# Rotary tables multiplied out on chip, n1 and pooled tiles in pairs, fold drains of 512 columns, and other scheduler constants: one change to an encoder kernel on eight cores

## The chip, the cores and the metric

One Trainium2 chip, all eight cores, each with two of the sixteen sequences and no traffic between cores. The metric is device time in microseconds of the slowest core. The chip has a second, slower state: in some executions the cores of one die run at a mean granted clock down to 0.83, the other die's stay at 0.99, and the time is 2276 to 2593 us, whatever the kernel. Such executions are left out here. Because the slowest of eight cores is a noisy figure, I also give the **mean of the eight cores** of one execution, averaged over the fast executions of a kernel.

## The reference

```python
n1 = rmsnorm(x, g_mix)
proj = n1 @ w_in                      # q, k, v, pooled branch, two gates
a = gqa_block_attention(rope(rms(q)), rope(rms(k)), v) @ w_attn_up
p = (multiscale_pool(u) @ pool_w * pool_scale) @ w_pool_up
h = x + (sig(g_a) * a + sig(g_p) * p) @ w_out
h = h + cross_attention(rmsnorm(h, g_cross), rmsnorm(mem, g_mem))   # 4 heads, 256 memory tokens
h = h + relu(rmsnorm(h, g_ffn) @ w_ff1) ** 2 @ w_ff2
return rmsnorm(h, g_final)
```

A sequence of 2048 is a grid of 32 rows and 64 columns; the rotary angle of half the dimensions follows the row, of the other half the column. So cos and sin tables are products of a row table and a column table.

## The kernel before

The program is written as a graph of operations. A list scheduler, run when the kernel is built, gives every operation to an engine and fixes the order on each engine, from a small model of what each costs. All loads and stores are issued by SyncE (SP), one queue, in the scheduled order. Eight blocks of 512 tokens pass; the raw f32 weights come in 228 loads of 512 KB (`wst`), are rounded to bf16 in one of ten W slots, and are stored to scratch (`wsc`) for the later blocks. The parts that the change touches:

```python
DMA_BW = 318.0                        # the scheduler's model of transfers
BACKLOG = 6000.0
...
def rope_tables(tb):
    for i in range(2):
        c = V("cs", "M1")
        load(lambda c=c: ap(c), rope_d[tb, i], 262144, [c], early=30000.0)
...
for kc in range(8):                   # n1 goes out in eight tiles of 128 KB
    store(n1d[s, tb, kc], lambda n=n: ap(n), 131072, [n], [dram(("n1", s, tb, kc))])
...
def fold_a(h, ch):                    # W_q and K of the memory folded into one matrix
    PE([mm(b, wsl(w, dt * 1024 + ch * 128), m[("XK", 2 * h + dt)], ...) for dt in range(2)], [b])
    for s in range(2):
        copy_any(At[s] [..., ch, :], b[:, s * 256:(s + 1) * 256], 256, ..., scale=g_cross[ch])
```

The softmax here doesn't subtract the row's maximum and nothing guards it: scores larger than these inputs give would overflow.

## Time and profile before

| kernel before | |
|---|---|
| time, slowest core | 2255.9 us median of the three first runs (2252.47 to 2256.78) |
| PE busy in the profiled run | 2140.6 of 2253.9 us, 95% |
| PE idle by stretch: 0-140, 140-260, 260-480, 480-560 us | 33, 22, 8, 12 us |
| period of the steady blocks | 245.7 us |
| moved by DMA, main queue | 440.6 MB |

PE is nearly always busy, so every gain without fewer matmuls must come out of its idle time, and most of that lies in the first 260 us. The lines of this profile are in the prediction.

### The profile page before, as it was taken

Reading aid. Unit: us, or ns where it says so; the run is one execution under the profiler, and the core shown is the slowest. Engines: PE = TensorE matmul, PEld = TensorE weight load, DVE = VectorE, ACT = ScalarE, POOL = GpSimd, SP = SyncE. Lnnn points to the kernel's source line nnn. Section 1 sums busy time; section 2 is a strip of 40 time slices with the busy share of each in tenths; the row PEclk is TensorE's granted clock in tenths of the full one; section 3 lists DMA queues with packets and bytes.
Section 4 is the critical chain, followed back from the end, with each engine's and each line's share of the span. In section 5 each row is a group of like instructions: output and inputs, shape, how many; then the busy total and the mean of one; then the engine's idle time right before and its main releaser. Section 6 shows DMA issues by size and latency. Waiting matters only on the chain.

```text
span 2253.9 us, 33704 instructions; the slowest of 8 cores (2242.3 to 2253.9 us)
## 1 busy us (share of the span) xinstructions
PE 2140.6 (95%) x10758; PEld 900.0 (40%) x10758; DVE 1471.4 (65%) x1793; ACT 1481.2 (66%) x1875; POOL 368.5 (16%) x273
## 2 busy tenths in 40 slices
PE   6788999988999999999999999999999999999997
PEld 3423333333444434444434443444434443444443
DVE  4688876667876687666774578557774687456502
ACT  6678777747786477853788368854786368835550
POOL 0112321124221241101110021002110122000100
PEclk9999999999999999999999999999999999999998
DMA  9957995989587992946633463435533463336342
GB/s 284 287 189 244 299 306 185 286 277 314 199 275 267 284 306 101 299 153 197 211 113 122 151 223 104 139 124 191 174 117 117 168 215 113 123 128 226 127 145 75
DMA packets 156267, 442.75 MB, mean 196 GB/s; under 512 B 17472, under 2 KB 38976, under 8 KB 156096
## 3 DMA queue, kind: packets, MB, share of 16 engines
q1 hardware_dynamic: 156096, 440.60, 60.7%
q8 instruction: 91, 1.49, 0.3%
q14 instruction: 80, 0.66, 0.1%
HBM read 376.57 MB, written 63.96 MB: 195 GB/s over the span
## 4 chain that ended last, share of the span: by engine, by line
PE 81%; DMA 6%; ACT 4%; DVE 4%; issue 3%; SPq 1%; POOL 0%; DVEq 0%; ACTq 0%; POOLq 0%
PE ps L603 81%; DMA M_p<-wst 3%; ACT M_p L1014 2%; DMA wsc<-W_p 1%; SPq L611 1%; DMA outT<-M_p 1%; SPq L615 1%; DMA M_p<-xT 1%; DVE M_p L1270 0%; DMA vec_sb<-vec 0%; ACT M_p L1241 0%; DVE M_p L1025 0%; ACT M_p L709 0%; DVE S_p L715 0%; ACT W_p L623 0%
## 5 line engine op out<-in xcount | busy, mean ns | idle before, releaser
L603 PE MATMUL ps<-S_p,W_p 128*128 128x512 bf16 x7680 | 1731.9, 381 | 33.1 <-DVE S_p L715 7.7
L603 PEld LDWEIGHTS ps<-S_p,W_p 128*128 128x128 bf16 x7680 | 733.7, 98 | 996.2 <-issue 160.3
L1014 ACT ACTIVATE M_p<-ps 128x2048 bf16<-128x2048 f32 x256 | 479.5, 1873 | 220.3 <-PE ps L603 215.9
L1025 DVE TENSOR_TENSOR M_p<-M_p 128x1024 f32<-128x1024 f32 x224 | 284.5, 1270 | 162.2 <-ACT M_p L1014 158.0
L1026 DVE TENSOR_TENSOR M_p<-M_p 128x1024 f32<-128x1024 f32 x224 | 309.6, 1382 | 17.4 <-DVE M_p L1025 0.9
L698 POOL TENSOR_TENSOR M_p<-M_p 128x512 f32<-128x512 f32 x67 | 101.3, 1512 | 806.3 <-ACT M_p L689 710.4
L689 ACT ACTIVATE M_p<-M_p 128x512 f32<-128x512 f32 x216 | 134.1, 625 | 137.2 <-DVE M_p L1222 47.0
L626 POOL CAST W_p<-M_p 128x1024 bf16<-128x1024 f32 x92 | 115.1, 1256 | 493.8 <-PE ps L603 291.8
L1241 ACT ACTIVATE M_p<-ps 128x512 f32<-128x512 f32 x256 | 151.6, 592 | 46.7 <-PE ps L603 45.2
L1257 DVE TENSOR_TENSOR M_p<-ps,M_p 128x512 f32<-128x512 f32 x64 | 44.2, 691 | 208.3 <-PE ps L603 208.3
L603 PE MATMUL ps<-S_p,KV_p 64*128 64x512 bf16 x1024 | 157.1, 385 | 15.4 <-ACT M_p L1014 14.8
L603 PE MATMUL ps<-M_p,KV_p 128*64 128x512 bf16 x1024 | 137.0, 389 | 16.6 <-ACT M_p L1014 12.3
L1245 ACT ACTIVATE S_p<-M_p 128x512 bf16<-128x512 f32 x220 | 138.6, 630 | 20.4
L623 ACT ACTIVATE W_p<-M_p 128x1024 bf16<-128x1024 f32 x71 | 74.4, 1051 | 108.1 <-PE ps L603 88.3
L1092 ACT ACTIVATE M_p<-ps,nbg 128x512 f32<-128x512 f32 x128 | 87.1, 685 | 58.7 <-PE ps L603 57.9
L603 PE MATMUL ps<-W_p,S_p 128*128 128x256 bf16 (+2 forms) x576 | 96.1, 318 | 4.0 <-ACT W_p L623 1.8
L603 PEld LDWEIGHTS ps<-M_p,KV_p 128*64 128x64 bf16 x1024 | 49.3, 110 | 96.7 <-issue 72.2
L626 DVE CAST W_p<-M_p 128x1024 bf16<-128x1024 f32 x61 | 42.7, 716 | 65.4 <-PE ps L603 29.2
L603 PEld LDWEIGHTS ps<-S_p,KV_p 64*128 64x128 bf16 x1024 | 29.6, 94 | 121.4 <-issue 121.3
L603 PE MATMUL ps<-S_p,ones_bf 128*128 128x512 bf16 x166 | 56.5, 403 | 19.0 <-ACT S_p L689 11.6
L603 PEld LDWEIGHTS ps<-W_p,S_p 128*128 128x128 bf16 x576 | 55.1, 100 | 43.6 <-issue 21.3
L1095 ACT ACTIVATE M_p<-M_p 128x1024 f32<-128x1024 f32 x64 | 67.5, 1055 | 4.1
(76 smaller groups left out, 1486.7 us busy)
## 6 DMA issues: line engine op xcount, KB each, us to landing
W_p<-wsc SPq DMA_DIRECT2D x383, 512.0 KB, 4.3
M_p<-wst SPq DMA_DIRECT2D x228, 512.0 KB, 9.8
wsc<-W_p SPq DMA_DIRECT2D x69, 512.0 KB, 9.3
M_p<-xT SPq DMA_DIRECT2D x128, 256.0 KB, 10.6
outT<-M_p SPq DMA_DIRECT2D x64, 256.0 KB, 4.7
M_p<-rope SPq DMA_DIRECT2D x32, 256.0 KB, 10.7
n1d<-S_p SPq DMA_DIRECT2D x56, 128.0 KB, 9.1
S_p<-n1d SPq DMA_DIRECT2D x56, 128.0 KB, 5.6
```

What stands on the lines that cost most here:

```text
L603: return e.matmul(out(), lhsT=lhsT(), rhs=rhs(), start=start, stop=stop, skip_group_check=True, **kw)
L623: return e.activation(out=dst(), in_=src(), func=AF.Copy)
L626: return e.tensor_copy(out=dst(), in_=src())
L689: A(lambda e: e.activation(out=ap(sq), in_=src(), func=AF.Square), 512, False, R, [sq])
L698: TT(lambda e: e.tensor_tensor(out=ap(out), in0=ap(acc), in1=ap(sq), op=ALU.add), [acc, sq], [out])
L1014: A(lambda e: e.activation(out=b16(P).rearrange("p (a n) -> p a n", n=512), in_=ps[:, 0:4, :], func=AF.Exp, scale=0.125), 2048, True, S, [P])
L1025: D(lambda e: e.tensor_tensor(out=ap(acc), in0=ap(acc), in1=lo(), op=ALU.add), 1024, [P, acc], [acc], port=True)
L1026: D(lambda e: e.tensor_tensor(out=ap(acc), in0=ap(acc), in1=hi(), op=ALU.add), 1024, [P, acc], [acc], port=True)
L1092: A(lambda e, b=b, i=i: e.activation(out=ap(Et)[:, i * 512:(i + 1) * 512], in_=ap(b), func=AF.Exp, bias=nbg[:, i * 8 + j:i * 8 + j + 1], s ...
L1095: A(lambda e: e.activation(out=ap(Et), in_=ap(Et), func=AF.Ln, bias=1.0, scale=1.0), 1024, False, [(Et, 0), (Et, 1)], [(Et, 0), (Et, 1)])
L1241: A(lambda e: e.activation(out=ap(rl), in_=ap(b), func=AF.Relu), 512, True, [b], [rl])
L1245: e.activation(out=ap(H), in_=ap(rl), func=AF.Square))
```

## The change

Four things: the rotary tables are no longer loaded but multiplied out from one table of 192 columns; n1 and pooled tiles are moved two at a time; the fold is drained 512 columns at a time for one sample, with its gain moved elsewhere; and the scheduler gets another model of transfers and other rules for SP.

```diff
-DMA_BW = 318.0
-BACKLOG = 6000.0
+DMA_BW = 385.0
+DMA_FIX = 200.0
+BACKLOG = 5000.0
 ...
-if best is not None and r > best[0] + 400.0 and r > s_min + 400.0:
+if best is not None and r > best[0] + (1600.0 if e == "sp" else 400.0) and r > s_min + 400.0:
 ...
-if best is None or c[0] < best[0]:
+if best is None or c[0] < best[0] or (e == "sp" and best[2].dma is not None and c[1] < best[2].U
+                                      and c[0] < best[0] + 1500.0):
 ...
-load(lambda c=c: ap(c), rope_d[tb, i], 262144, [c], early=30000.0)
+TT(lambda e, c=c, i=i: e.tensor_tensor(out=ap(c) as [8 rows, 64 columns],
+    in0=rope[:, row table], in1=rope[:, column table], op=ALU.mult), [CONST["rope"]], [c])
 ...
-for kc in range(8):
-    store(n1d[s, tb, kc], lambda n=n: ap(n), 131072, ...)
+for k2 in range(4):
+    store(n1d[s, tb, k2], lambda v=v: b16(v), 262144, [(v, 0), (v, 1)], ...)
 ...
-for s in range(2):
-    copy_any(..., 256, [b, CONST["vec"]], [(At[s], ch)], scale=g_cross, engs=("act", "dve"))
+copy_any(..., 512, [b], [(At[s], c2)], engs=("act", "dve"))
 ...
-rounded(j, None)
+rounded(j, C_GCROSS)
```

(Cut: the same change for pooled tiles and for the loads; the host's tables; pool sizes M1 24 to 32 and S1 70 to 52; the model of GpSimd's time.)

## The prediction

> **What bounds the kernel now.** I read the page's header first: engines, the forty slices, the chain. TensorE (PE) is busy 95% of 2253.9 us, and the chain runs through it for 81%.
>
> ```profile
> PE 2140.6 (95%) x10758; PEld 900.0 (40%) x10758; DVE 1471.4 (65%) x1793; ACT 1481.2 (66%) x1875; POOL 368.5 (16%) x273
> ...
> PE   6788999988999999999999999999999999999997
> ...
> DMA  9957995989587992946633463435533463336342
> ...
> PE 81%; DMA 6%; ACT 4%; DVE 4%; issue 3%; SPq 1%; POOL 0%; DVEq 0%; ACTq 0%; POOLq 0%
> ```
>
> All that can be won without removing matmuls is PE's idle time, 2253.9 - 2140.6 = 113 us, plus what a lowered clock costs. The slices put the idle time at the start, where the DMA row shows 9s. So next I asked for busy times in seven stretches (columns: PE, weight load, DVE, ACT, POOL, granted clock, DMA share, GB/s):
>
> ```profile
> 0.00:140.00 140.00, 106.84 (x582) 52.71 (x583) 83.64 (x139) 94.72 (x149) 17.21 (x19) 0.91 0.99 289
> 140.00:260.00 120.00, 98.30 (x505) 33.99 (x504) 103.72 (x125) 92.89 (x107) 24.73 (x20) 0.97 0.67 216
> 260.00:480.00 220.00, 211.50 (x1048) 86.35 (x1046) 157.70 (x181) 161.88 (x196) 57.08 (x43) 0.99 0.85 268
> 480.00:560.00 80.00, 67.99 (x309) 28.37 (x309) 59.51 (x81) 54.19 (x68) 28.22 (x22) 0.94 0.97 297
> 560.00:1100.00 540.00, 529.81 (x2775) 231.69 (x2774) 385.79 (x478) 364.83 (x471) 108.56 (x82) 1.00 0.72 233
> 1100.00:2029.00 929.00, 918.30 (x4593) 375.33 (x4591) 598.09 (x674) 617.52 (x743) 119.56 (x80) 1.00 0.44 146
> 2029.00:2254.00 225.00, 207.90 (x957) 91.56 (x955) 82.95 (x119) 95.16 (x143) 13.11 (x10) 0.97 0.43 143
> ```
>
> PE's idle time by stretch is 33, 22, 8, 12, 10, 11 and 17 us. From 1100 to 2029 us, 41% of the run, PE is 99% busy at clock 1.00: nothing in this change removes PE work there, so that stretch should stay. Up to 140 us DMA is 99% busy. From 140 to 260 DMA has room (0.67), but DVE is at 86%; this is attention of the first block beside the fold of W_q and K. The third look was at the waits in 140 to 190 us, and at the groups that drain the fold:
>
> ```profile
> PE ps L603 <- ACT M_p L1014: 10.0, 9, 1.9
> ...
> PE ps L603 <- DVE W_p L627: 3.6, 4, 1.3
> ```
>
> ```profile
> L627 DVE TENSOR_SCALAR W_p<-ps,vec_sb 128x256 bf16<-128x256 f32 x33 | 14.7, 478 | 3.9 <-PE ps L603 2.0 <-DMA wsc<-W_p 1.3
> ...
> L624 ACT ACTIVATE W_p<-ps,vec_sb 128x256 bf16<-128x256 f32 x31 | 13.3, 476 | 3.6 <-DVE W_p L627 1.5 <-DMA wsc<-W_p 1.2 <-PE ps L603 0.4
> ```
>
> There PE waits for the attention exponential on ACT (L1014), which queues behind fold drains, and for drains themselves. The DMA issues show what will go:
>
> ```profile
> M_p<-rope SPq DMA_DIRECT2D x32, 256.0 KB, 10.7
> n1d<-S_p SPq DMA_DIRECT2D x56, 128.0 KB, 9.1
> S_p<-n1d SPq DMA_DIRECT2D x56, 128.0 KB, 5.6
> ```
>
> **What the Trainium skill says.** "Perfetto Trace Analysis", DMA Optimizations, says: "Small DMAs (< 2KB) have significant per-transfer overhead." The n1 and pooled tiles move as 1 KB rows. The trace agrees: in stretches where their stores prevail DMA makes 267 GB/s (50 to 58 us) and 254 (88 to 98), against 320 at 24 to 34 us, at a DMA share of 1.0 throughout. "SBUF — State Buffer", Who interferes with whom, says that GpSimd (POOL) and a DVE instruction with two SBUF inputs contend for a shared port held for a whole instruction. The trace agrees in that the same DVE add L1026 takes 1.23 us mostly but 1.87 once beside a POOL cast (170 us), and its mean is 1.382. "TensorE: Matmul & The Clock Gate", Part 1, has PE at half rate until it has been busy some 3.4 us. Here eight 512-column matmuls took 3.62 us just after a 5.3 us wait (101.9 us) against 1.89 otherwise, and the granted clock at 110 to 120 us was 0.63. "VectorE: DVE Perf Modes", on the TRN2 errata, gives each instruction a fixed part beside its elements. Here a 256-wide drain costs DVE 0.478 us and a 512-wide one 0.684, less than twice; so merging two drains pays.
>
> **The change part by part.**
>
> Rotary tables. Thirty-two loads of 262 KB (8.4 MB of 440.6) become one of 98 KB and 32 products of 128x512. The order of the changed program gives 29 of these to POOL and 3 to DVE. On POOL a 128x512 f32 tensor-tensor takes 1.27 us alone and 1.51 on average (L698): 29 x 1.27 to 1.51 = 37 to 44 us, on an engine 16% busy, on the path only where a rotation waits for its table. On DVE 3 x 0.75 (L1258) = 2.2 us. On the path lies DMA in the first 140 us: ten of the loads fall there, 2.62 - 0.10 = 2.52 MB, at 289 GB/s 8.7 us of queue time. Of the others two fall near 212 us, four at 473 to 536 us, the rest mostly where DMA has room.
>
> Pairs. n1 and pooled moves fall from 168 to 84, each twice as long, rows 2 KB. With the table loads, issues fall by 31 + 84 = 115, from 1084 to 969. In the first 140 us there are 24 + 12 stores of 131 KB, 4.7 MB: at 260 GB/s 18.1 us, at an assumed 305 15.5, so 2.7 us (estimate). M1 grows from 24 to 32 slots and S1 shrinks from 70 to 52. A block's eight n1 and four pooled tiles then take six M1 slots where they took twelve of S1, so prefetch depth hardly changes.
>
> Fold. Per pair of chunks four drains of 256 become two of 512, without the gain. The order gives 14 to DVE and 18 to ACT: 14 x 0.684 + 18 x 0.600 = 20.4 us, against 14.7 + 13.3 = 28.0 by the busy columns (30.5 by count times mean, which keeps overlaps). So 8 to 10 us less on two engines that are both near 85% there, about 4.5 us off the stretch if it shortens evenly. Matmuls rise by 64 but keep their columns: under 1 us. The order also shows 100 fold matmuls in one run, where before an attention visit came after every four to six; PE can stream them but will wait if W_q is late.
>
> Gain moved. The gain g_cross goes into the rounding of h after W_out, 64 instructions that POOL can no longer take. ACT: from 18 x 0.706 + 30 x 0.615 = 31.2 to 70 x 0.706 = 49.4 us, +18.2; DVE 35.4 to 34.8; POOL -15.0. That is 2.3 us more ACT per block, in steps where PE has eight 512-column matmuls per rounding and ACT is near 66%: off the path, apart from some 0.1 us at each stage end.
>
> Scheduler constants. They have SP choose among loads differently and can move any transfer. Two holes in DMA of 20 us (140 to 160 and 340 to 360 us, where SP waited for a slot) could close. The PE order changes throughout, but mode switches hardly: 657 to 653. I give this no sum, only width.
>
> Sum, on the path: first 140 us: 8.7 + 2.7 = 11.4 us of transfers. PE idles 33 us there, of which 14 precede the first projection (18.3 us) and depend on the first x loads, which stay first in the queue. I let 8 of 11.4 through. Clock: 0.91 in that stretch costs 0.09 x 140 = 13 us; fewer long waits may return 2. Fold: 4.5. At 473 to 560 us: four table loads gone, 1.05 MB at 297 GB/s or 3.5 us, and eight n1 and four pooled loads paired, some 0.5 us (estimate): 4. Rest of the head (260 to 480, 560 to 1100): 3. Port contention from 29 products: DVE loses perhaps 29 x 0.3 = 9 us, a tenth of it on the path, -1. Total 8 + 2 + 4.5 + 4 + 3 - 1 = 20.5; 2255.9 - 20.5 = 2235.
>
> **Rivals.** (a) The transfers are hidden anyway: DVE and ACT bound the head once DMA is lighter, only the fold counts. For: DVE at 86% after 140 us. Against: ACT waited 13.7 us and DVE 17.3 for raw weights before 107 us. It gives about 2249. (b) POOL's products hold the shared port and delay DVE in its busiest stretch, and a late table stalls a rotation. For: the 1.23 to 1.87 us spread. Against: POOL is under 21% busy in every early stretch, and tables can be made early. About 2258. (c) The long fold run waits for W_q: eight raw halves must be converted first. For: DMA was saturated until 140 us. Against: the lighter queue brings them some 11 us sooner. About 2245. (d) The new load choice closes the DMA holes as well, and later DMA-bound stretches (240 to 330, 480 to 560 us) start ahead: 15 to 25 us more, about 2215.
>
> **Range and chances.** Idle time outside the steady stretch is 102 us, 14 of it at the very start and 17 in the last stretch, untouched. Faster by over 2% needs 45 us of the remaining 71: only (d) at its best, 0.09. Slower by over 2% needs a new wait in the repeated blocks: 0.02. Within 2%: 0.89. The range 2213 to 2250 holds (a), (c) and most of (d).
>
> **What would show it.** DMA bytes near 432.3 MB, 969 issues. PE idle before 140 us down from 33 to about 23, and the start of the fold about 8 us sooner; fold drains 20 us in all; idle at 480 to 560 us from 12 to about 8; blocks in the steady stretch still 245.7 us apart (1156.66, 1402.34, 1648.00 in the chain). I am wrong if that period moves by over 1 us, if PE waits above 3 us inside the fold run, or if rotations wait on POOL.

## The result, and the profile after

The changed kernel takes **2252.3 us** (median of 4 runs, 2251.99 to 2252.76); the kernel before in the same comparison 2254.18 (4 runs, 2251.19 to 2256.78). The ratio is 0.9992, 95% interval 0.9975 to 1.001. (A ratio is the mean time of one kernel's fast runs over that of the other's of the same rounds, so not quite the ratio of the medians quoted.) The class "same" was right, the size was not: 20 us were predicted, at most 2 came, and 2252.3 lies outside the range of 2213 to 2250.

The page of the changed kernel's slowest core: busy times, the slices of PE and of DMA, what the main queue moved, and the chain by engine.

```profile
PE 2138.2 (95%) x10822; PEld 906.4 (40%) x10822; DVE 1469.2 (65%) x1754; ACT 1492.0 (66%) x1883; POOL 419.4 (19%) x304
...
PE   7978899989999999999999999999999999999997
...
DMA  9976976999496882935633462435533463336342
...
q1 hardware_dynamic: 139536, 432.30, 58.8%
...
PE 80%; DMA 7%; DVE 4%; ACT 3%; issue 3%; SPq 1%; POOL 0%; DVEq 0%; ACTq 0%; POOLq 0%
```

The bytes went as foreseen (432.30 MB), and the DMA row has lost some of its 9s at the front. Its hole moved from 140-160 to 125-141 us. By stretches (columns as in the prediction):

```profile
0.00:140.00 140.00, 112.94 (x655) 56.61 (x656) 102.48 (x151) 101.78 (x154) 44.12 (x39) 0.96 0.89 272
140.00:260.00 120.00, 96.47 (x521) 37.53 (x519) 89.91 (x97) 85.31 (x94) 32.16 (x25) 0.94 0.79 244
260.00:480.00 220.00, 207.78 (x1040) 83.71 (x1037) 158.76 (x179) 163.87 (x198) 50.93 (x38) 1.00 0.80 258
480.00:560.00 80.00, 71.94 (x336) 30.57 (x337) 64.03 (x86) 57.74 (x74) 27.21 (x20) 0.98 0.97 310
```

PE is 6.1 us busier before 140 us (112.94 against 106.84). Then it is 1.8 us less busy to 260 and 3.7 less to 480 us. The gain of the head arrives, and part of it leaks out again. I also looked at the chain of waits from some 90 to 260 us; first the kernel before, then the changed one:

```profile
by line: PE ps L603 54.3%; ACT M_p L1014 10.1%; issue 8.1%; DMA wsc<-W_p 8.1%; DMA M_p<-wst 6.8%; SPq L611 3.6%; DVE W_p L627 3.5%; ACT W_p L623 2.1%; ACT W_p L624 2.0%; DVE W_p L626 1.0%; DVE S_p L1035 0.8%; DVE M_p L1026 0.7%; DVE M_p L10
```

```profile
by line: PE ps L613 44.5%; DMA M_p<-wst 17.2%; ACT M_p L1031 8.9%; issue 6.1%; DMA M_p<-n1d 5.8%; DMA wsc<-W_p 4.1%; ACT W_p L633 4.1%; DVE W_p L636 2.1%; DVE M_p L636 1.5%; SPq L621 1.4%; DVE M_p L1042 1.2%; DVE M_p L1043 0.7%; DVE M_p L75
```

Two things are not to be read out of this pair. The 256-column drains L624 and L627 (5.5%) are not gone but have become 512-column ones on L633 and L636, the lines that also round weights: drains and rounding together hold 8.6% before (L623, L624, L626, L627) and 6.2% after. And the raw weight's transfer, 6.8% against 17.2%, differs as much between the cores of one kernel: it is 27.8% on core 0 of the kernel before, and in the second pair of profiles, r_before and r_after, 6.5 and 7.2%. In the waits at 140 to 190 us, where the prediction had found 10.0 us for the exponential and 3.6 for drains, the changed kernel shows:

```profile
PE ps L613 <- ACT M_p L1031: 8.1, 3, 3.8
PE ps L613 <- DVE W_p L636: 1.1, 3, 0.5
```

Nine short waits for the exponential became three longer ones, with fewer attention visits in the window. (In the second pair of profiles it is 11.1 us in nine waits against 6.5 in four.) The fold itself starts some 10 us sooner, at 133 to 134 us where its first drain came at 143 to 144, and is through at 159 us instead of 187 (means of cores).

**Where the lead goes.** Marks in the traces, mean of the eight cores, each kernel profiled twice (us). The last column is an experiment told below, the kernel before with the rotary bytes taken out at unchanged order.

| mark | before | after | difference | x_bytes, difference |
|---|---|---|---|---|
| first attention exponential of block 0 | 104.8 | 95.5 | -9.3 | -5.4 |
| its 32nd and last | 242.8 | 243.1 | +0.3 | -5.1 |
| end of block 0 | 516.1 | 512.0 | -4.1 | -4.4 |
| end of block 3 | 1313.4 | 1309.4 | -4.0 | -6.4 |
| end, mean of cores | 2244.1 | 2240.3 | -3.8 | -6.4 |

Nine microseconds of lead at the first exponential are nothing at the 32nd and four at the end. The first two rows are clear of the scatter; the lower ones less so, because the two profiles of the kernel before end 6.5 us apart (2247.3 and 2240.8), those of the changed one 0.6. The runs below put the change's gain in the mean of cores at 1.6 us. In the same traces PE's idle time, counted as all gaps of more than 0.45 us up to a time, mean of eight cores and of two profiles:

| up to | 140 us | 200 us | 260 us | 373 us | 480 us | 800 us |
|---|---|---|---|---|---|---|
| before | 27.0 | 40.9 | 46.0 | 51.5 | 55.5 | 64.6 |
| after | 24.3 | 32.8 | 44.7 | 49.2 | 55.7 | 62.3 |
| x_bytes | 23.7 | 36.6 | 42.0 | 47.8 | 54.3 | 60.9 |

At 200 us the changed kernel has saved 8.1 us of idle time. Between 200 and 260 us it gives 6.8 of them back. The threshold matters a little: with every gap counted the lead is 9.0 us at 200, 3.2 at 260, 1.5 at 480 and 3.3 at 800 us.

### The profile page after: what moved, and what is told of

Same layout as the page of the kernel before. It is cut to its first block, busy times and chain, and to the rows that moved or that the text cites. A ratio compares the mean times of both kernels' runs of the same rounds, so it can differ in the third digit from the quotient of the medians.

```text
span 2251.2 us, 33586 instructions; the slowest of 8 cores (2229.4 to 2251.2 us)
## 1 busy us (share of the span) xinstructions
PE 2138.2 (95%) x10822; PEld 906.4 (40%) x10822; DVE 1469.2 (65%) x1754; ACT 1492.0 (66%) x1883; POOL 419.4 (19%) x304
## 3 DMA queue, kind: packets, MB, share of 16 engines
q1 hardware_dynamic: 139536, 432.30, 58.8%
## 4 chain that ended last, share of the span: by engine, by line
PE 80%; DMA 7%; DVE 4%; ACT 3%; issue 3%; SPq 1%; POOL 0%; DVEq 0%; ACTq 0%; POOLq 0%
PE ps L613 80%; DMA M_p<-wst 4%; DMA wsc<-W_p 1%; ACT M_p L1031 1%; SPq L621 1%; DVE M_p L725 1%; DMA outT<-M_p 1%; DMA M_p<-xT 1%; ACT W_p L633 1%; DVE M_p L1286 1%; DMA M_p<-n1d 0%; DVE M_p L636 0%; ACT M_p L720 0%; DVE M_p L1042 0%; DVE M_p L1043 0%
## 5 line engine op out<-in xcount | busy, mean ns | idle before, releaser
L613 PE MATMUL ps<-S_p,W_p 128*128 128x512 bf16 (+1 forms) x6144 | 1370.6, 378 | 19.2 <-ACT W_p L633 5.7
L613 PEld LDWEIGHTS ps<-S_p,W_p 128*128 128x128 bf16 x6144 | 585.0, 98 | 772.2 <-issue 109.8
L613 PE MATMUL ps<-M_p,W_p 128*128 128x512 bf16 x1600 | 380.6, 386 | 10.6 <-DVE M_p L725 5.6
L709 POOL TENSOR_TENSOR M_p<-M_p 128x512 f32<-128x512 f32 x72 | 111.7, 1552 | 811.2 <-ACT M_p L700 778.2
L613 PEld LDWEIGHTS ps<-M_p,W_p 128*128 128x128 bf16 x1600 | 153.9, 99 | 218.2 <-issue 48.5
L636 POOL CAST W_p<-M_p 128x1024 bf16<-128x1024 f32 x96 | 122.0, 1277 | 425.9 <-PE ps L613 232.3
L633 ACT ACTIVATE W_p<-M_p 128x1024 bf16<-128x1024 f32 x71 | 74.1, 1054 | 113.0 <-PE ps L613 73.2
L636 DVE CAST W_p<-M_p 128x1024 bf16<-128x1024 f32 x57 | 42.7, 771 | 57.4 <-DMA M_p<-wst 22.8
L613 PE MATMUL ps<-W_p,M_p 128*128 128x384 bf16 (+1 forms) x512 | 76.9, 305 | 0.0
## 6 DMA issues: line engine op xcount, KB each, us to landing
W_p<-wsc SPq DMA_DIRECT2D x383, 512.0 KB, 4.2
M_p<-wst SPq DMA_DIRECT2D x228, 512.0 KB, 9.0
wsc<-W_p SPq DMA_DIRECT2D x69, 512.0 KB, 8.8
```

Of the source, the lines that this page charges most:

```text
L613: return e.matmul(out(), lhsT=lhsT(), rhs=rhs(), start=start, stop=stop, skip_group_check=True, **kw)
L633: return e.activation(out=dst(), in_=src(), func=AF.Copy)
L636: return e.tensor_copy(out=dst(), in_=src())
L709: TT(lambda e: e.tensor_tensor(out=ap(out), in0=ap(acc), in1=ap(sq), op=ALU.add), [acc, sq], [out])
```

## The experiments

Eighteen kernels ran. First the parts, each alone on the kernel before. "Mean" is the mean of the eight cores over the fast runs; the difference is to the kernel before's fast runs. "Slowest" is the longest core's span, averaged likewise; the device times of which the text gives medians are about 1.5 us longer. "Plan" is the length that the scheduler itself computes while the kernel is built; it is 2224.5 for the kernel before and 2217.5 for the changed one. "96th" is the time at which the 96th raw weight load is issued, and the last column is the end minus that, both means of cores in the profiled run.

| run | what it is | plan | mean | difference | slowest | 96th | end - 96th |
|---|---|---|---|---|---|---|---|
| p_rope | before + rotary products | 2220.1 | 2241.7 | +0.1 | 2249.0 | 375 | 1864 |
| p_pairs | before + pairs | 2214.7 | 2235.9 | -5.7 | 2244.6 | 370 | 1866 |
| p_fold | before + fold | 2223.3 | 2239.1 | -2.5 | 2246.7 | 367 | 1870 |
| p_sched | before + scheduler | 2229.7 | 2249.6 | +8.0 | 2260.5 | 382 | 1869 |
| n_sched | after without scheduler | 2231.9 | 2249.2 | +6.9 | 2259.4 | 375 | 1876 |
| n_fold | after without fold | 2216.3 | 2243.9 | +1.6 | 2255.3 | 377 | 1869 |
| n_rope | after without rotary products | 2213.6 | 2239.5 | -3.7 | 2253.5 | 373 | 1865 |
| r_after | after | 2217.5 | 2240.8 | -1.6 | 2250.5 | 373 | 1867 |
| c_lot | before, model nudged by 0.1 ns | 2227.9 | 2248.0 | +5.7 | 2257.5 | 380 | 1869 |
| x_bytes | before, rotary bytes out, order kept | (2224.5) | 2235.4 | -7.8 | 2245.0 | 373 | 1866 |
| x_bytes2 | the same again | (2224.5) | 2238.9 | -7.0 | 2247.2 | 375 | 1861 |
| r_before | before | 2224.5 | 2242.6 | -0.6 | 2249.9 | 379 | 1862 |
| d_after | after, stores later in SP's order | (2217.5) | 2278.3 | +35.1 | 2288.1 | 411 | 1868 |
| a_s97 | after, model nudged by 2 ns | 2215.9 | 2242.4 | -3.5 | 2251.1 | 373 | 1867 |
| a_s93 | after, model nudged by -2 ns | 2224.3 | 2255.2 | +9.3 | 2263.8 | 388 | 1868 |
| a_m29 | after, model nudged by 0.4 ns | 2217.3 | 2242.9 | -3.0 | 2253.2 | 373 | 1870 |
| p_rope24 | p_rope, model nudged by -0.1 ns | 2211.9 | 2237.1 | -8.8 | 2245.1 | 370 | 1868 |
| a_bytes | after, idle copies added, order kept | (2217.5) | 2274.9 | +29.0 | 2284.1 | 392 | 1882 |

(Two to six fast runs each, p_sched one. The mean of one execution scatters by about 2 us either way. p_sched was in the slow state four times; the undisturbed dies of three of these had means of 2249 to 2252. One fast run of p_sched, 2283.34 us, and one of n_rope, 2277.10, lie far off their own others, with two cores at a clock of 0.97, and are left out of these means. With them the differences would be +11.4 and -2.3; and 2265.12 of n_rope, which shows the same clock, was kept. The 96th load and the end of p_sched are those of its undisturbed die.)

**Each part alone.** The edits are the four parts of the diff above, one each.

> The kernel before with the rotary products alone (tables of 32 and 64 columns multiplied out on chip, nothing else of the change). My prediction's sum put some 8 us on the first 140 us, three quarters of it for these bytes: so if the transfers of the head were the bound and nothing takes it back, the slowest core ends 5 to 8 us sooner, at about 2247 us. If the gain of the head is eaten between the first attention exponential and the end of block 0's attention (as in the whole change, where the first exponential came 10 us sooner and the 32nd at the same time), the first exponential comes about 5 to 8 us sooner and the end is within 3 us. If the rotary products on GpSimd hold VectorE up, the steady blocks are longer by over 1 us each and the end later.

> The kernel before with n1 and pooled tiles in pairs alone. No bytes go, only 92 of the transfers; by the prediction 2 to 3 us of the head. Head-bound theory: end 2 to 3 us sooner. Theory that it only reshuffles the order of the schedule: anything within 5 us either way, with the mean of the eight cores moving as little as the slowest.

> The kernel before with the fold's drains at 512 columns alone (two chunks at a time, one tile of the pair of samples). The prediction gave it 4.5 us plus 2 us of clock. If the drains bound the fold, the end of block 0's attention (mean of cores) comes 4 to 7 us sooner. If the fold waits for raw weights instead (theory of the transfers), the wait moves from the drain lines to the casts of raw weights and the end of block 0's attention stays within 2 us.

> The kernel before with the new constants and rules of the list scheduler alone (transfer rate 385 plus 200 ns each, backlog 5000, SyncE may look 1600 ns ahead, GpSimd's time). The prediction gave it 3 to 4 us of gain at 473 to 560 us and in the rest of the head. Theory that the new constants are too fast for this chip and place casts and loads too early: the chain from 90 to 260 us then carries over 10% on a raw weight's transfer instead of 7%, and block 0's attention ends no sooner or later. Theory that any change of order moves the end by 5 us at random: no pattern.

Measured: medians of 2250.41, 2245.82, 2248.88 and one undisturbed run of 2262.02. The rotary products alone brought nothing where the prediction had most; pairs brought 5.7; the new constants cost 8.0 where 7 of gain had been booked. In p_sched the first exponential came early (96.5 us on the undisturbed die) and the 32nd late (245.8). The four differences sum to -0.1, the whole change has -1.6. (The 92 transfers of the expectation on p_pairs are 84.) At this point the constants looked guilty.

**The whole without one part, and a control.**

```diff
# c_lot, on the kernel before
-MM_FIX = 2.5
+MM_FIX = 2.6
```

> The whole change with the scheduler's old constants and rules. In the first four runs the three other parts each took 1 to 6 us off the mean of the eight cores and off the end of block 0's attention (238 to 240 us against 244), and the new constants alone added some 8 us. If the new constants are what eats the gain, this kernel's mean of cores is 2228 to 2234 us and its slowest core about 2238 to 2243; if the three gains overlap (each removes the same wait), it stays at 2235 to 2238 in the mean; if the long fold run (no attention visit for 19 us) eats it, the run is still there and the mean stays at 2241.

> The whole change with the old fold (256-column drains), new scheduler constants. If the fold's form causes the long run without attention visits and with it the loss, the gap of 19 us in the visits goes and the mean of cores falls from 2241 to 2236 or less. If the scheduler's constants are the cause, the end of block 0's attention stays at 243 us or comes later and the mean stays at 2241 to 2246.

> The changed kernel again, unedited, so that the means of its cores come from the same chip as the other runs: slowest core 2252 us, mean of cores 2240 to 2243, one core of each pair 8 to 15 us behind the other.

> The kernel before with one irrelevant figure of the scheduler's model nudged (a fixed cost per matmul of 2.6 ns instead of 2.5): no work changes, 161 lines of PE's order do. If any nudge moves the end by 5 us or more (lottery), the mean of cores differs from the kernel before's by that much, and the differences of the four parts run so far prove little; if the mean stays within 2 us, they are effects.

Taking the new constants away did not free the gain: n_sched is 8.4 us slower than r_after in the mean. The same constants cost 8 us on the kernel before and win 8 in the changed one, so the theory that they eat the gain by themselves falls. n_fold is not faster either (+1.6). The control is the reason to distrust all of these: a figure of the model nudged by 0.1 ns, no work changed, and the mean is 5.7 us up (ratio 1.003, 1.0012 to 1.0048). Adding a part means a new order of everything, and an order alone is worth as much as a part. What a part is worth has to be measured with the order held.

**The order held.** The loads keep their planned size, so the schedule does not move; a comparison of the instruction lists showed PE, DVE, ACT and POOL the same row by row.

```diff
# x_bytes, on the kernel before (result wrong on purpose)
-load(lambda c=c: ap(c), rope_d[tb, i], 262144, [c], early=30000.0)
+load(lambda c=c: ap(c)[:, 0:32], rope_d[tb, i][:, 0:32], 262144, [c], early=30000.0)
-in1=ap(cs[0])
+in1=ap(cs[0])[:, 0:32].unsqueeze(1).to_broadcast([128, 16, 32])      # and cs[1]
# d_after, on the changed kernel, after scheduling: each scratch store planned before 400 us
+delay_stores(order, 3, 400000.0)   # moves it behind up to 3 later SP issues, if no user comes first
```

> The kernel before in exactly its own order on PE, VectorE, ScalarE, GpSimd and SyncE, with each rotary load cut from 512 to 32 columns (the rotations read those 32 columns again and again; the result is wrong on purpose). The scheduler still plans with the full size, so nothing moves; only the bytes go. By the prediction's term (8 us of the first 140 us, three quarters of it these bytes) the first attention exponential comes 5 to 8 us sooner and the end 5 to 6 us sooner in the mean of the cores. If the transfers are hidden anyway because buffers come free no sooner, the 16th and 32nd raw weight load are issued sooner but the 64th and 96th within 2 us of the kernel before's, and the end within 2 us.

> The kernel before, unedited, for a second profile on the same chip, because the one profiled first was slower (mean of cores 2247 us) than its later executions (2240 to 2244): first attention exponential at 105 us, 32nd at 240 to 243, end of block 0 at 513 to 516, mean end 2242.

> The changed kernel with each store of a weight tile to scratch that is planned in the first 400 us moved behind up to three later SyncE issues, as far as buffers allow (32 stores, 79 places), all other engines in the same order. If loads wait behind stores in SyncE's order (head-of-line), the SyncE waits for the fold's last drain (16.6 us once) shrink, the 64th and 96th raw load come 3 to 8 us sooner and the end 3 to 6 us sooner. If the loads wait for buffers, not for the order, the 96th raw load stays within 1 us and the end within 2 us.

> The whole change with the rotary tables still loaded (4.1 MB more of transfers). By the prediction's sum it must be about 6 us slower than the changed kernel. If order decides more than bytes, it follows the length that the scheduler itself plans for it: that plan is 2213.6 us here, 2217.5 for the changed kernel and 2224.5 for the kernel before, and the six variants run so far with old constants came 16 to 22 us over their plans in the mean of cores, those with new constants 20 to 28: so 2234 to 2241 in the mean, as fast as the changed kernel or faster in spite of the bytes. If the rotary products on GpSimd disturb VectorE, it is faster too, and then the block period falls by over 0.5 us.

x_bytes is the clean measurement: 7.8 us in the mean of cores (2235.4 against 2243.2), ratio of the slowest 0.9971 (0.9938 to 1.0003). The first exponential comes 5 us sooner in its profile and that lead stays through every mark. Its 16th, 96th and 160th raw loads are 3 to 7 us earlier. (The comparison with the reference passed although the tables were wrong; that says that it is loose, not that they were right.) The reads of 32 columns instead of 512 are no rival: the two VectorE operations that take the tables cost 61.4 us in x_bytes and 61.6 in r_before. So the transfers of the head are not hidden, and what they are worth is what the prediction said, if the order stays.

d_after was to show that loads wait behind stores in SP's order. It went the other way: 35 us slower than the kernel before, 37 slower than the changed one. Waits of PE (220 to 345 us) and of SP (140 to 345 us) in d_after, then of SP in r_after; columns are total, times, longest:

```profile
PE ps L638 <- DVE W_p L661: 10.9, 4, 6.6
PE ps L638 <- ACT M_p L1056: 9.8, 5, 6.0
PE ps L638 <- ACT S_p L771: 7.3, 1, 7.3
```

```profile
SPq L510 <- DVE M_p L1068: 43.9, 7, 15.8
...
SPq L507 <- DMA wsc<-W_p: 21.5, 3, 8.4
```

```profile
SPq L482 <- DMA wsc<-W_p: 9.5, 4, 3.7
```

A finished fold or weight tile sits in its W slot until its store has landed, so a later store frees the slot later, and SP then waits for stores to land (21.5 us against 9.5; over the eight cores it is 20 to 25 against 8 to 14). The theory that the stores block the loads is refuted; they are, if anything, needed early. n_rope, with 8.3 MB more to move than the changed kernel (not the 4.1 of its expectation), is not slower than it in the mean (-3.7 against -1.6, or -2.3 with the run left out): order outweighs the bytes again.

**Is it the long fold run?** In the changed kernel the visits of block 0's attention stop for 20 us (135 to 156 us) while 100 fold matmuls run, which was a rival in the prediction. Its own nudges offer orders with and without that stop, and with an early or late 96th raw load, from the same parts.

```diff
-SWITCH = 95.0          # the changed kernel
+SWITCH = 97.0          # a_s97;  93.0 in a_s93;  MM_FIX 2.5 to 2.9 in a_m29
-MM_FIX = 2.5           # p_rope
+MM_FIX = 2.4           # p_rope24
```

> The changed kernel with one figure of the scheduler's model nudged (cost of a change of PE's mode 97 ns instead of 95). Its own plan puts the 32nd attention exponential at 221 us instead of 230, with no gap over 9 us between visits, but the 96th raw weight load at 358 instead of 359 us, and the end at 2215.9 instead of 2217.5. If the long fold run is what takes the gain back, the end comes 6 to 9 us sooner than the changed kernel's (mean of cores 2241): 2232 to 2235. If the 96th raw load decides, the end is within 3 us of it: 2238 to 2243.

> The changed kernel with that figure at 93 ns. Its plan keeps the long fold run and the 32nd exponential (229 us) but puts the 96th raw weight load at 367 us, 8 later, and the end at 2224.3. If the fold run alone decides, its mean of cores stays at 2241 within 2 us. If the 96th raw load decides, it is 5 to 9 us later: 2246 to 2250.

> The changed kernel with the fixed cost per matmul at 2.9 ns: a second order without the long fold run (32nd exponential planned at 220 us, largest gap 7 us) and the 96th raw load at 356 us, 3 sooner. Fold run theory: 2231 to 2235 in the mean, as a_s97. Raw load theory: 2236 to 2239.

> Rotary products alone with a fixed cost per matmul of 2.4 ns; plan: 32nd exponential at 222 us, 96th raw load at 352 us (before 365), end at 2211.9 against 2220.1 of the same part at 2.5 and 2224.5 of the kernel before. If the plan's order is worth what it says on the chip, 10 us below the kernel before, about 2231 to 2234 in the mean of cores and 2241 on the slowest: faster than the changed kernel with three of its parts left out. If order is noise that plans do not see, 2241 as p_rope.

The 32nd exponential did come 8 us sooner in a_s97 and a_m29 (234.9 and 234.1 against 242.6), with no stop over 12.2 us. But the end of block 0 was at 511.7 and 511.9 against 511.8, and the whole is 2 us better at most against their own runs of the kernel before, within scatter. So the long fold run is not what took the gain. Nor is the idle time between 200 and 260 us alone: a_s97 and a_m29 give back 7.2 and 8.3 us there where the changed kernel idles 11.9, and by 260 us have idled 40.8 and 39.3 us in all against its 44.7, yet they end no sooner. Meanwhile a_s93, whose 96th raw load was planned 8 us later, issued it 15 us later and ended 15 us later in the profile. In its waits from 260 to 345 us, and its chain from 290 to 345:

```profile
PE ps L613 <- ACT W_p L633: 7.1, 1, 7.1
PE ps L613 <- ACT M_p L1031: 4.2, 2, 2.7
```

```profile
by line: PE ps L613 50.2%; DMA wsc<-W_p 32.6%; issue 7.6%; ACT M_p L1031 3.4%; DVE M_p L1180 2.7%; DVE W_p L636 2.5%; DVE S_p L637 2.3%; ACT W_p L633 1.9%; DVE M_p L709 1.1%; DVE M_p L1042 0.8%; SPq L621 0.6%; DVEq L485 0.3%; DVEq L482 0.2%
...
286.62 12.29 DMA wsc<-W_p
```

PE waits once for 7.1 us for a weight being rounded on ACT, and the chain leads to a scratch store that had to land before a slot was free. All eight cores show such stores in this stretch of the chain, 18 to 44% of it; in a_s97 none has a share worth listing there. This looks like the mechanism of d_after, in an order that came about by itself. Its cost is 11 us by the differences to the kernel before (+9.3 against -1.6), 15 by the profiles; that it is this store and nothing else in the order was not tested.

The table's last column carries this further: in sixteen of the eighteen kernels the end comes 1861 to 1870 us after the 96th raw weight load is issued, whether that is at 367 or at 411 us. Of the three kernels that are late there by 15 us and more, a_s93 and d_after end late by as much, a_bytes by more. For the small gains in question the rule is too coarse: its scatter of 9 us is as large as they are, and the changed kernel and x_bytes, whose 96th loads come at 374 us, end 2.6 us apart in their profiles. The mark that is sharp comes later. From the end of block 3 to the end all eighteen kernels, the kernel before and the changed one take 929.8 to 931.6 us (mean of cores); from the end of block 0 they still take 1724 to 1742. What a kernel has gained or lost by 1310 us is what it ends with.

**Are the bytes hidden in the new order?**

```diff
# a_bytes, on the changed kernel; ahead of 16 x loads and 14 n1 loads, 8 of them before 51 us
+e.dma_start(out=dmy[s, tb, i], in_=memT[i]).then_inc(dsm, 16)     # 256 KB, read by nobody
```

> The changed kernel in exactly its own order, with the removed rotary bytes put back as 30 idle copies of 256 KB each (from one DRAM tensor to a scratch one that nobody reads) issued on SyncE just ahead of the x loads and n1 loads, 8 of them in the first 51 us. Additive theory: the bytes cost here what they gained in x_bytes, so the first attention exponential comes 5 to 8 us later than the changed kernel's 95.5 us and the mean of cores is 5 to 8 us later than its 2241: 2246 to 2249. Theory that the new order hides them: the exponential may come later, but the 96th raw load and the end stay within 2 us (2240 to 2243).

> The kernel before at its own order with the rotary loads cut to 32 columns, repeated unedited from x_bytes with five rounds: if the 7.8 us stand, mean of cores 6 to 9 us under the kernel before of the same call; if the profiled execution of x_bytes (2 us) was the truer one, 1 to 3 us.

x_bytes2 gives 7.0 us in the mean and a ratio of 0.9959 (0.9932 to 0.9986): the byte gain stands. a_bytes costs some 31 us against r_after (+29.0 against -1.6, from different calls), with the first exponential 15 us later, so the new order does not hide these transfers. But the dose was too strong and in the wrong place. Two copies stand among the first three transfers, where the first rotary load of the kernel before had been issued at 10 us; behind them, from 3 to 11 us, the DMA engines moved 182 GB/s where those of r_after moved 290; and 22 of the 30 came after the head. It speaks against "hidden" without settling it; it does not give the size of the byte gain inside the new order.

**The leak seen closely.** PE busy (second column after the length) from 0 to 200 and from 200 to 260 us, first r_before, then r_after, then x_bytes2, each on its slowest core:

```profile
0.00:200.00 200.00, 152.52 (x834) 68.25 (x835) 135.88 (x205) 146.13 (x210) 31.37 (x28) 0.94 0.85 259
200.00:260.00 60.00, 52.22 (x266) 18.63 (x265) 52.96 (x64) 43.72 (x50) 14.15 (x12) 1.00 0.82 264
```

```profile
0.00:200.00 200.00, 164.23 (x932) 79.84 (x946) 141.00 (x190) 144.29 (x199) 63.04 (x55) 0.94 0.87 264
200.00:260.00 60.00, 46.88 (x233) 15.66 (x234) 51.31 (x57) 43.87 (x49) 12.38 (x10) 0.94 0.80 244
```

```profile
0.00:200.00 200.00, 157.53 (x851) 70.16 (x852) 140.10 (x210) 148.33 (x214) 33.68 (x30) 0.93 0.83 253
200.00:260.00 60.00, 53.49 (x272) 19.51 (x271) 53.41 (x64) 44.79 (x52) 13.94 (x12) 1.00 0.82 256
```

The changed kernel is 11.7 us ahead of r_before at 200 us and loses 5.3 of it in the next 60. x_bytes2 is 5.0 ahead and loses nothing. What PE waits for there, r_before and then r_after (200 to 262 us):

```profile
PE ps L603 <- ACT M_p L1014: 3.0, 4, 1.2
PE ps L603 <- DVE W_p L626: 2.0, 2, 1.6
```

```profile
PE ps L613 <- ACT M_p L1031: 6.7, 6, 1.3
PE ps L613 <- DVE W_p L636: 2.6, 3, 1.2
PE ps L613 <- ACT M_p L720: 2.3, 1, 2.3
```

The last fourteen attention visits take 51 to 54 us in r_before, r_after and a_s97 alike. In the new order PE had done early the fold (through at 159 us instead of 187) and other work that used to fill the time between a visit's scores and its exponential; that it now waits for the exponential for this reason is my reading, no run tests it. In a_s97, without the long run, PE idles 7.2 us there and ends no better.

## Why the prediction was wrong, point by point

**Rotary bytes and pairs, 8 us let through of 11.4: right in size, wrong in that it would stay.** The bytes alone are worth 7.0 to 7.8 us in the mean of cores at the old order, close to the term. In the changed kernel the first exponential came 9.3 us sooner. PE's idle time before 140 us was to go from 33 to 23 us on the slowest core; it went to 27.1. The start of the fold was to come 8 us sooner and came some 10 us sooner.

**The failed step is the one on the scheduler constants and the order: "I give this no sum, only width."** The sum adds each part as if the order of all other work stayed, and the order is not neutral. From the same parts it makes 12.8 us between a_s97 and a_s93, 5.7 us between the kernel before and c_lot, and about 9 us between p_rope and p_rope24, each against its own runs of the kernel before. The order that came with this change gives back 6.8 us of PE's idle time between 200 and 260 us, and the lead of 9.3 us at the first exponential is gone at the 32nd, where the same bytes at held order still had 5.1. Which property of the order costs this stays open: taking the long fold run away did not bring the gain back. The width allowed was mostly below the estimate (rival d); rivals a and b were the right side.

**Rest of the head 3 us, 473 to 560 us 4 us: not seen at the end.** The idle time of the slowest core at 480 to 560 us did fall from 12 to 8.1 us. But from 373 to 480 us the changed kernel idles 6.5 us against 4.0, so the idle time saved is 2.3 us at 373, nothing at 480 and 2.3 again at 800: the second stretch only gives back what the first had taken.

**Fold, 4.5 us and 2 us of clock: the drains as computed, the gain not shown.** They cost 14 x 0.685 + 18 x 0.599 = 20.4 us, as foreseen, and PE's wait at 140 to 190 us for VectorE's drains (3.6 us) is 1.1, rounding of weights included. The clock term was too small: the granted clock before 140 us rose from 0.91 to 0.96, which by the prediction's own reckoning is 0.05 x 140 = 7 us. Alone the fold brought 2.5 us, which is less than what c_lot shows that a nudge can do; its true worth stays open. The sign I named for being wrong, a wait of over 3 us inside the fold run, came close: the longest was 2.9 us.

**Port contention, -1: nothing seen.** The 29 products took 37.1 us on POOL (1.294 each), no VectorE wait for one of them is in the profile, and the block period is 245.5 against 245.7 us. The DVE add of the prediction's example has a mean of 1.403 us against 1.382, but 1.420 in n_rope, which has no products, and 1.378 in p_rope, which has.

**The metric.** In the mean of cores the change gains 1.6 us (r_after) to 3.8 (the two pairs of profiles). On the slowest core it gains nothing that is clear of noise; the two cores of a pair ended 13.6 us apart (12.3 in the first comparison) against 9.1 in the kernel before. The prediction reasoned on one core. Why the spread grew was not tested.

**Rivals.** (a) "Hidden anyway" named the time best (2249) but its reason is refuted by x_bytes. (c), the long fold run, existed, 20 us without a visit, but taking it away did not help. (b) and (d) did not happen.

**What stays open.** Which store or load in the new order costs most: d_after and a_s93 point to a mechanism (a scratch store that lands late holds a W slot), not to its share in the changed kernel. How the 7 us of the bytes and the loss divide inside the changed kernel is inferred from different orders, not measured. The best version found is p_rope24, the rotary products alone with a lucky order: 2247.77 us median, ratio 0.9955 (0.9925 to 0.9984) to the kernel before. It is faster than the kernel before by far less than 2%.

## What to carry to other kernels

When a scheduler decides the order, a change is two changes; run a control in which only an irrelevant figure of its model moves, and measure a part with the order held before believing its gain or loss. Follow a lead by marks through the trace: a lead at one mark counts only if it is still there at the mark after which everything runs at a fixed pace, here the end of block 3. One profile of a kernel is not enough for that: two of the same kernel ended 6.5 us apart.

## What the Trainium skill lacked or had wrong

- "TensorE: Matmul & The Clock Gate", Part 1, under Seeing it yourself, says that a peak-current limiter takes a whole die to 13/16 of the clock once three of its cores run dense matmuls, and to budget 1.95 GHz. Here all eight cores ran with PE 98 to 99% busy from 1100 to 2029 us at a granted clock of 1.00, and twenty 512-column matmuls took 4.48 us, 2.29 GHz by that. In the slow executions one die had a mean clock of 0.83 to 0.97 and the other 0.98 to 0.99, and fast and slow executions came from the same kernel. The page lacks an all-core kernel that runs without the limit; whether the slow state is this limit coming and going was not tested.
- "HBM Reference", Specifications, gives each core of a pair the same share when both stream. The page has nothing on how far the two may drift apart: the runs show them 6 to 17 us apart at the end, averaged over the four pairs of an execution, with the side changing from one execution to the next. Whether memory causes it was not tested.
- No page says how much a fixed order of instructions is worth by itself: 5.7 to 12.8 us of 2250 here, for a nudge of 0.1 to 2 ns in a scheduler's model.
